# Row spread by TensorE for the first norm, later transposes, output's norms moved, and another product order in one chunk

## The chip, the core and the metric

The kernel runs on one core of one Trainium2 chip. The metric is the device time of the whole program in microseconds (us); less is better. The core has five engines with a queue of instructions each: TensorE (PE, with PEld for its weight loads), VectorE (DVE), ScalarE (ACT), GpSimd (POOL) and SyncE (SP), which here only issues DMAs. Each engine works its queue in order; an instruction that needs another engine's result or a DMA's data waits on a semaphore, and all that stands behind it in the queue waits with it.

## The reference

One layer of a decoder for 512 tokens of width 1024, fp32: FFN with half weight, token mixer, FFN with half weight, each between two RMS norms.

```python
def rms_norm(x, g):
    xf = x.astype(jnp.float32)
    y = xf * lax.rsqrt(jnp.mean(xf * xf, axis=-1, keepdims=True) + EPS)
    return (y * g.astype(jnp.float32)).astype(x.dtype)

def swiglu(h, w_gu, w_down):                 # w_gu 1024 x 5632, w_down 2816 x 1024
    gate, up = jnp.split(h @ w_gu, 2, axis=-1)
    return (jax.nn.silu(gate) * up) @ w_down
...
h = swiglu(rms_norm(x, ffn1_pre[l]), ffn1_w_gu[l], ffn1_w_down[l])
x = x + 0.5 * rms_norm(h, ffn1_post[l])
h = token_mixer(rms_norm(x, mix_pre[l]), ...)
x = x + rms_norm(h, mix_post[l])
h = swiglu(rms_norm(x, ffn2_pre[l]), ffn2_w_gu[l], ffn2_w_down[l])
x = x + 0.5 * rms_norm(h, ffn2_post[l])
```

The mixer projects to 512 pooling channels and to q (8 heads of 64), k and v (2 heads each). The pooling half takes causal means over 2, 4, 8 and 16 tokens; the attention half is causal over 128 tokens with rotary position and a sink per head. Each half is normed, and one output projection follows.

## The kernel before, in words

**Numbers.** An fp32 operand is held as two reduced fp32 parts, hi and lo: ACT copies hi (L166, L398, L438), DVE or POOL subtracts it from the source to get lo (L172, L401, L439). A product is three TensorE products, hi·hi, lo·hi and hi·lo, summed in PSUM (`mm3`, L364 to L366, and `product_late`, L480 to L483, which takes hi·lo last). PSUM has eight banks of 128 x 512 fp32.

**Tokens.** x lies in four tiles of 128 tokens. For a norm, ACT squares and sums a tile (`squares`, L358; half of it on DVE at the start, L353), DVE makes the mean (L344), POOL the root (`power`, L339), and DVE multiplies by root and gain, in two halves (`scaled`, L383). The result is called xn_a (first FFN), xn_b (mixer) and xn_c (second FFN). TensorE transposes it (tr_f L429, tr_mx L392), and ACT and DVE split the transposed tile into hi and lo.

**FFN.** The 2816 hidden columns are worked in 11 chunks of 256, gate and up together. Chunk 0 runs as eight blocks of 24 products (two token halves, gate and up, two column halves; each over two halves of the input width), called (i, kh) with i from 0 to 7. `gate_up` calls a hook, `between(i, kh)`, ahead of each half block: for the first FFN `first_steps` (L822), which norms and transposes x there, for the second `last_steps` (L1348), which runs the whole mixer and the output projection at (0, 0) and the last two transposed tiles between the blocks. Chunks 1 to 10 use seven products of half-size blocks each, numbered 1 to 7, on sums of weight blocks a, b, c, d (DVE, L224: `f_1s` = c + d and so on) and on sums of token blocks (`token_sums`, f1f and f1t). Their results go to three pairs of banks, x, y and z, taken in turn from four pairs. Then `down_proj` multiplies by w_down, again in seven products, on single banks; at its start it takes two banks for x, where chunk 10's pairs were.

**Weights.** `W` loads weights ahead over SP's queue into eight buffers and splits them into hi and lo, into a ring of six. Its list has a fixed order; `W.get` and `W.more` say when the next entries are made, and `W.put` on which engines.

**Mixer and output.** `qkv_block(t)` gives q (`pq`, 24 products of 128 x 512) and k, v (`pkv`, 24 of 128 x 256) for token tile t, with some other work between the two. `output` makes the output projection for each tile in four gathers of 12 products (`po`), adds the two halves into hm (ACT for attention, DVE L1286 for pooling), norms the sum (root r_mo, gain g4 at L1290), adds it to x (L1345) and starts the second FFN's norm (xn_c).

**Order.** TensorE's order is the order of the code throughout. Within `in_order()` this holds for DVE, ACT and POOL as well; that covers the start, the first four blocks of chunk 0 in both FFNs with all that their hooks do (so the mixer and the output too), and the down projections. Elsewhere a scheduler orders these engines, with `behind` keeping an instruction after a given one.

**Start.** SP loads tile 0 of x, the first half of the first gain, broadcast to 128 partitions (L291), tile 1, the second half, and then the first weights, with tiles 2 and 3 between them. TensorE multiplies zeros (`idle_work`, L791) until the first tile is normed.

## Time and profile before

| what | us |
|---|---|
| median of three runs | 844.01 (843.72 to 845.08) |
| the profiled execution | 843.83 |
| its span, first to last instruction | 841.9 |
| DVE busy in the span | 662.7 (79%) |
| DVE, weight splits L172 (84 of 128x1024) | 94.8 |
| mean granted clock of TensorE in the span | 0.995 |

The profile is one execution: its own time is the 843.83, and the span lies within it. Rows name line, engine, operation, output and inputs, with buffer numbers left out; "[3.54 <-DVE xn_b]" means that the engine stood idle for 3.54 us before the row, and that DVE's write of xn_b ended it. A matmul's duration is longer than the distance from one start to the next, since they are pipelined; so TensorE's pace is read from starts. The granted clock is the share of full speed that TensorE was allowed.

### The profile page before, as it was taken

Reading aid. Unit: us, or ns where it says so; the run is one execution under the profiler, and the core shown is the slowest. Engines: PE = TensorE matmul, PEld = TensorE weight load, DVE = VectorE, ACT = ScalarE, POOL = GpSimd, SP = SyncE. Lnnn points to the kernel's source line nnn. Section 1 sums busy time; section 2 is a strip of 40 time slices with the busy share of each in tenths; the row PEclk is TensorE's granted clock in tenths of the full one; section 3 lists DMA queues with packets and bytes.
Section 4 is the critical chain, followed back from the end, with each engine's and each line's share of the span. In section 5 each row is a group of like instructions: output and inputs, shape, how many; then the busy total and the mean of one; then the engine's idle time right before and its main releaser. Section 6 shows DMA issues by size and latency. Waiting matters only on the chain. (4 is left out here: it accounts for less than half of the span.)

```text
span 841.9 us, 14062 instructions
## 1 busy us (share of the span) xinstructions
PE 819.0 (97%) x5525; PEld 750.6 (89%) x5525; DVE 662.7 (79%) x856; ACT 470.1 (56%) x743; POOL 207.8 (25%) x291
## 2 busy tenths in 40 slices
PE   7999999999999999899999998999999999999996
PEld 5999999999988888788878878999999999988885
DVE  6987787777989877944766779877877778798875
ACT  6654444445556656636886467444444445566661
POOL 3103344433310000233532011133333334300001
PEclk9999999999999999999999999999999999999999
DMA  9428888988896666411005402278898888967622
GB/s 301 134 86 224 241 225 226 230 238 240 235 282 199 208 203 200 154 40 51 26 26 151 148 27 76 76 215 235 223 231 235 239 225 226 265 221 211 204 87 100
DMA packets 96877, 150.77 MB, mean 179 GB/s; under 512 B 6948, under 2 KB 53676, under 8 KB 96812
## 3 DMA queue, kind: packets, MB, share of 16 engines
q1 hardware_dynamic: 77100, 103.74, 39.3%
q0 software_dynamic: 19712, 46.15, 23.4%
q8 instruction: 43, 0.70, 0.3%
q14 instruction: 22, 0.18, 0.1%
HBM read 147.77 MB, written 48.23 MB: 233 GB/s over the span
## 5 line engine op out<-in xcount | busy, mean ns | idle before, releaser
L172 DVE TENSOR_TENSOR f_d_lo<-f_d_raw,f_d_hi 128x1024 fp32r<-128x1024 f32 x84 | 94.8, 1131 | 25.3 <-ACT f_d_hi L166 25.3
L571 POOL DMA_DIRECT2D f_t<-in_ffn_w_down x132 | 89.6, 755 | 81.7 <-issue 49.7
L166 ACT CAST f_d_hi<-f_d_raw 128x1024 fp32r<-128x1024 f32 x84 | 80.0, 979 | 26.9 <-PE f_z L366 10.6
L595 ACT COPY f_h<-f_y 128x512 f32<-128x512 f32 x20 | 11.7, 587 | 75.6 <-PE f_y L366 75.6
L568 POOL COPY f_k<-f_h 1x1 f32<-1x1 f32 x18 | 21.0, 1166 | 130.0 <-DVE f_h L560 130.0
L603 ACT ACTIVATE f_s<-f_s 128x1024 f32<-128x1024 f32 x20 | 21.2, 1060 | 41.4 <-DVE f_s L602 41.4
L571 POOL DMA_DIRECT2D f_t<-f_t x44 | 32.1, 796 | 37.8 <-issue 29.1
L600 ACT COPY f_s<-f_x 128x512 f32<-128x512 f32 x20 | 11.7, 587 | 45.1 <-PE f_x L366 45.1
L364 PE MATMUL f_x<-f_d_hi,f1e_hi 128*128 128x512 f32 x88 | 34.5, 392 | 0.7 <-DVE f_h L611 0.7
L364 PE MATMUL f_x<-f_d_hi,f2e_hi 128*128 128x512 f32 x88 | 34.4, 390 | 0.7 <-DVE f_h L611 0.7
L365 PE MATMUL f_x<-f_d_lo,f1e_hi 128*128 128x512 f32 x88 | 34.3, 389 | 0.0
L366 PE MATMUL f_x<-f_d_hi,f1e_lo 128*128 128x512 f32 x88 | 34.3, 389 | 0.0
L365 PE MATMUL f_x<-f_d_lo,f2e_hi 128*128 128x512 f32 x88 | 34.3, 389 | 0.0
L366 PE MATMUL f_x<-f_d_hi,f2e_lo 128*128 128x512 f32 x88 | 34.2, 389 | 0.0
L587 ACT COPY f_s<-f_x 128x512 f32<-128x512 f32 x20 | 11.7, 587 | 39.9 <-PE f_x L366 29.8
L637 ACT CAST f2e_hi<-f_h 128x1024 fp32r<-128x1024 f32 (+1 forms) x21 | 20.5, 979 | 20.4 <-DVE f_h L629 4.8
L637 ACT CAST f1e_hi<-f_h 128x1024 fp32r<-128x1024 f32 (+1 forms) x21 | 20.5, 980 | 20.2 <-DVE f_h L629 4.8
L339 POOL TENSOR_TENSOR r_f1po<-ms_f1po,half 128x1 f32<-128x1 f32 x4 | 2.5, 628 | 106.9 <-DVE ms_f1po L344 106.9
L339 POOL TENSOR_TENSOR r_f2po<-ms_f2po,half 128x1 f32<-128x1 f32 x4 | 2.5, 628 | 104.3 <-DVE ms_f2po L344 104.3
L364 PE MATMUL po<-wo_hi,yT_hi 128*128 128x512 f32 x64 | 25.3, 395 | 0.0
L638 DVE TENSOR_TENSOR f1e_lo<-f_h,f1e_hi 128x1024 fp32r<-128x1024 f32 (+1 forms) x21 | 23.6, 1131 | 2.1 <-ACT f1e_hi L637 2.1
L638 DVE TENSOR_TENSOR f2e_lo<-f_h,f2e_hi 128x1024 fp32r<-128x1024 f32 (+1 forms) x21 | 23.6, 1132 | 2.1 <-ACT f2e_hi L637 2.1
(1027 smaller groups left out, 3416.2 us busy)
## 6 DMA issues: line engine op xcount, KB each, us to landing
f_t<-in_ffn_w_down POOLq DMA_DIRECT2D x132, 256.0 KB, 6.4
f_d_raw<-f_t SPq DMA_DIRECT2D x40, 512.0 KB, 4.4
f_d_raw<-in_ffn_w_down SPq DMA_DIRECT2D x30, 512.0 KB, 4.3
f_t<-f_t POOLq DMA_DIRECT2D x44, 256.0 KB, 6.7
f_raw<-in_ffn_w_gu SPq DMA_DIRECT2D x8, 512.0 KB, 8.4
x<-in_x SPq DMA_DIRECT2D x4, 512.0 KB, 8.6
f_d_raw<-f_t SPq DMA_DIRECT2D x8, 256.0 KB, 3.5
wq_raw<-in_w_in SPq DMA_DIRECT2D x4, 512.0 KB, 4.0
```

The costliest lines, as they stand in the source:

```text
L166: nc.scalar.copy(hi, src)
L172: return lambda: engine.tensor_tensor(lo, src, hi.bitcast(F32), ALU.subtract)
L364: nc.tensor.matmul(ps, wh, xh, start=first, stop=False, skip_group_check=open_)
L365: nc.tensor.matmul(ps, wh, xlo, start=False, stop=False, skip_group_check=open_)
L366: nc.tensor.matmul(ps, wlo, xh, start=False, stop=last, skip_group_check=open_)
L568: then = nc.gpsimd.tensor_copy(tick, hs[(c - 1) // 4][:1, 0, (c - 1) % 4, :1]).ins
L571: nc.gpsimd.dma_start(to, part, accum_op=op, max_dma_last_dim=2048)
L587: on_act.append(nc.scalar.copy(sg[:, :, a], px[:, :, a]).ins)
L595: on_act.append(nc.scalar.copy(h[1], py[:, :, a]).ins)
L603: on_act.append(nc.scalar.activation(sg, sg, AF.Silu, scale=-1.0).ins)
L637: nc.scalar.copy(hi, src)
L638: nc.vector.tensor_tensor(lo, src, hi.bitcast(F32), ALU.subtract)
```

## The change

Four places are changed.

1. Start: the first gain comes as one row of 1024 numbers (4 KB, on ACT's DMA queue) instead of two broadcasts to 128 partitions on SP's. TensorE spreads it, as a product of a column of ones with the row, into two PSUM banks, and xn_a reads it there. 14 products of zeros become 4 ahead of this and 2 behind.
2. Chunk 1 of both FFNs: loads in the order a, b, c, d (a, c, d, b before) and products in the order 1 2 5 6 3 7 4 (1 5 2 6 3 7 4 before). The list is made up to product 5 at once behind chunk 0 (`make_to`), and in the second FFN not before the last split of a transposed tile (`hold`).
3. Mixer: block 0's pkv follows its pq at once; tile 2's transposes stand behind pq of block 1, and tile 3's behind its pkv.
4. Output: DVE's mean and root for the output norm come right behind those of the second FFN's norm, and xn_c ahead of the gain at hm; the transposes of tiles 0 and 1 are later by two gathers each, their fp32 copies (`keep`) later still; two weight splits move into `output`, with DVE in place of POOL for lo.

```diff
 SUMS = 10
-WARM = 14
+WARM = 4
...
         key = {i: f"{name}_{c}{i}" for i in ("a", "b", "c", "d", "s1")}
-        for i in "acdb":
+        for i in "abcd" if c == 1 else "acdb":
             need[i] = W.add_load(key[i], src[i], shape)
...
-        for p, last, make in (
-            (1, "a", lambda: raw[key["a"]]), (5, "d", s1), (2, "b", lambda: raw[key["b"]]),
-            (6, "b", lambda: plus("a", "s1", "a")), (3, "b", lambda: plus("b", "a", "b")),
-            (7, "b", lambda: raw[key["c"]]), (4, "b", lambda: raw[key["d"]]),
-        ):
-            W.add(f"{name}_{c}p{p}", make, need=need[last])
+        make = {
+            1: lambda: raw[key["a"]], 5: s1, 2: lambda: raw[key["b"]], 6: lambda: plus("a", "s1", "a"),
+            3: lambda: plus("b", "a", "b"), 7: lambda: raw[key["c"]], 4: lambda: raw[key["d"]],
+        }
+        last = {1: "a", 5: "d", 2: "b"}
+        for p in (1, 2, 5, 6, 3, 7, 4) if c == 1 else (1, 5, 2, 6, 3, 7, 4):
+            W.add(f"{name}_{c}p{p}", make[p], need=need[last[p]] if p in last else max(need.values()))
...
+    g1row = wk.tile([1, D], F32, tag="sg2", bufs=2, name="g1row")
+    nc.scalar.dma_start(g1row, ffn1_pre[0:1, :])
     load_x(0)
-    g1 = [slot(f"g1{n}") for n in range(2)]
-    for n in range(2):
-        nc.sync.dma_start(g1[n], ffn1_pre[0:1, n * 512 : (n + 1) * 512].to_broadcast([P, 512]))
-        if n == 0:
-            load_x(1)
+    load_x(1)
+    onerow = wk.tile([1, P], F32, tag="ra", bufs=1, name="onerow")
+    nc.vector.memset(onerow, 1.0)
+    g1 = []
     warm = cp.tile([1, 2], F32, name="warm")
...
         nc.scalar.mul(hi[:, :, at], src, -1.0)
-        nc.vector.scalar_tensor_tensor(
+        return nc.vector.scalar_tensor_tensor(
             lo[:, :, at], src, -1.0, hi[:, :, at].bitcast(F32), ALU.mult, ALU.subtract
-        )
+        ).ins
...
-    def gate_up(name, xq, hs, between):
+    def gate_up(name, xq, hs, between, hold=lambda: []):
...
         W.run_ahead = 3
-        W.more(2)
+        with behind(hold()):
+            W.make_to(W.index[f"{name}_1p5"] + 1)
...
         last = None
-        on_act, on_dve = [], []
+        on_act, on_dve = [], [done.ins]
...
                     begin = [on_act[-2], on_dve[-1]]
-            py = bank_pair(f"{name}_y{c}")
-            product(py, a, operand(f"{nm}5"), xs_[5], last=False)
-            on_act.append(nc.scalar.copy(h[1], py[:, :, a]).ins)
-            pz = bank_pair(f"{name}_z{c}")
-            product(pz, a, operand(f"{nm}2"), xs_[2])
-            on_dve.append(nc.vector.tensor_tensor(sg[:, :, a], pz[:, :, a], sg[:, :, a], ALU.add).ins)
+            for p in (2, 5) if c == 1 else (5, 2):
+                if p == 5:
+                    py = bank_pair(f"{name}_y{c}")
+                    product(py, a, operand(f"{nm}5"), xs_[5], last=False)
+                    on_act.append(nc.scalar.copy(h[1], py[:, :, a]).ins)
+                    continue
+                pz = bank_pair(f"{name}_z{c}")
+                product(pz, a, operand(f"{nm}2"), xs_[2])
+                on_dve.append(nc.vector.tensor_tensor(sg[:, :, a], pz[:, :, a], sg[:, :, a], ALU.add).ins)
             product(px, a, operand(f"{nm}6"), xs_[6], False, False)
...
     idle_work(WARM)
+    for n in range(2):
+        g1.append(bank(f"g1{n}"))
+        nc.tensor.matmul(g1[n], onerow, g1row[:, n * 512 : (n + 1) * 512], start=True, stop=True)
+    idle_work(2)
     early = {}
...
             norm1(2)
+            qkv_block(0, lambda: None)
+            qkv_out(0)
             add_to_x(3)
             size1(3)
-            qkv_block(0, lambda: turn1(2))
             root1(3)
...
         nc.gpsimd.tensor_tensor(wpl, wpr, wph.bitcast(F32), ALU.subtract)
-        qkv_out(0)
         pcols = bank("pcols")
...
         nc.vector.tensor_tensor(cols[:, 4:8], cols[:, 0:4], cols[:, 4:8], ALU.mult)
-        qkv_block(1, lambda: transposes(3, xns[3], xT2, "mx"))
+        qkv_block(1, lambda: turn1(2))
+        turn1(3)
         qkv_out(1)
...
         for kh in range(2):
-            evacuate(later[t, kh], t, kh, xq2)
+            later["evac"] = evacuate(later[t, kh], t, kh, xq2)
...
             keep(later[t, kh], t, kh, xq2)
+
+    def after(t):
+        if t:
+            root_late(t - 1)
+        later["rr"] = power(mean_square(sums[t], EPS, f"mo{t}"), f"mo{t}")
+        if t:
+            normed(t - 1)
...
                 xq2.extend(quarters("f2"))
-            if t >= 2:
-                turn_late(t - 2)
+            if t == 3:
+                turn_late(1)
             if t:
                 later["ss", t - 1] = sizes(t - 1, "c")
-            if t >= 2:
-                keep_late(t - 2)
-            pool_part(t, 1, gather(t, 1, 0), (lambda: root_late(t - 1)) if t else (lambda: None))
-            if t:
-                normed(t - 1)
-            rr = power(mean_square(sums[t], EPS, f"mo{t}"), f"mo{t}")
+            if t == 3:
+                W.more(2)
+            pool_part(t, 1, gather(t, 1, 0), lambda: after(t))
+            if t == 3:
+                lows = [W.begin(), W.begin()]
+                keep_late(0)
             for n in range(2):
...
                 nc.vector.scalar_tensor_tensor(
-                    xs[t][:, at], hm[t, n], rr, xs[t][:, at], ALU.mult, ALU.add
+                    xs[t][:, at], hm[t, n], later["rr"], xs[t][:, at], ALU.mult, ALU.add
                 )
+            if t == 2:
+                turn_late(0)
+        return lows
...
             mixer()
-            output()
+            lows = output()
             later["ss", 3] = sizes(3, "c")
+            keep_late(1)
+            for low in lows:
+                low()
             root_late(3)
-            W.put(nc.scalar, nc.gpsimd)
             normed(3)
-            W.put(nc.scalar, nc.vector)
-            W.put(nc.scalar, nc.gpsimd)
-            W.put(nc.scalar, nc.vector)
         if (i, kh) == (1, 0):
             turn_late(2)
+        if (i, kh) == (2, 0):
+            W.run_ahead = 3
+            W.more(1)
+        if (i, kh) == (3, 1):
+            turn_late(3)
             keep_late(2)
-        if (i, kh) == (3, 0):
-            turn_late(3)
             keep_late(3)
     hs2 = []
-    ends = gate_up("f2", xq2, hs2, last_steps)
+    ends = gate_up("f2", xq2, hs2, last_steps, lambda: [later["evac"]])
     g6 = gain(ffn2_post, "g6")
```

On TensorE the mixer's start reads as follows before (pq0 and pkv0 are block 0's; tr_mx20 and tr_mx21 the transposes of tile 2's halves, tr_mx30 and tr_mx31 tile 3's; three dots stand for the rest of a block):

```order
L366 MATMUL pq0_3969<-wq3_hi_3857,xT2_3_lo_3830 128x512
L392 MATMUL tr_mx20_3994<-ident_101,xn_b2_3959 128x128 x4
L392 MATMUL tr_mx21_4003<-ident_101,xn_b2_3959 128x128 x4
L364 MATMUL pkv0_4012<-wkv0_hi_3892,xT2_0_hi_3823 128x256
...
L366 MATMUL pkv0_4012<-wkv1_hi_3955,xT2_3_lo_3830 128x256
L1173 MATMUL pcols_4058<-ident_101,rows_110 128x12
L364 MATMUL pq1_4062<-wq0_hi_3742,xT2_0_hi_3823 128x512
...
L366 MATMUL pq1_4062<-wq3_hi_3857,xT2_3_lo_3830 128x512
L392 MATMUL tr_mx30_4087<-ident_101,xn_b3_4042 128x128 x4
L392 MATMUL tr_mx31_4096<-ident_101,xn_b3_4042 128x128 x4
L364 MATMUL pkv1_4105<-wkv0_hi_3892,xT2_0_hi_3823 128x256
```

and with the change (lines are numbered two to ten further on):

```order
L368 MATMUL pq0_3958<-wq3_hi_3853,xT2_3_lo_3826 128x512
L366 MATMUL pkv0_3983<-wkv0_hi_3888,xT2_0_hi_3819 128x256
...
L368 MATMUL pkv0_3983<-wkv1_hi_3951,xT2_3_lo_3826 128x256
L1183 MATMUL pcols_4036<-ident_101,rows_110 128x12
L366 MATMUL pq1_4040<-wq0_hi_3738,xT2_0_hi_3819 128x512
...
L368 MATMUL pq1_4040<-wq3_hi_3853,xT2_3_lo_3826 128x512
L394 MATMUL tr_mx20_4065<-ident_101,xn_b2_3955 128x128 x4
L394 MATMUL tr_mx21_4074<-ident_101,xn_b2_3955 128x128 x4
L366 MATMUL pkv1_4083<-wkv0_hi_3888,xT2_0_hi_3819 128x256
...
L368 MATMUL pkv1_4083<-wkv1_hi_3951,xT2_3_lo_3826 128x256
L394 MATMUL tr_mx30_4109<-ident_101,xn_b3_4030 128x128 x4
L394 MATMUL tr_mx31_4118<-ident_101,xn_b3_4030 128x128 x4
```

Block 0's pkv has moved ahead of all transposes of tile 2, which now stand where tile 3's stood.

On DVE, in `output`, from the add into x of tile 2 to the second FFN's norm of the same tile (xn_c20, xn_c21), before (ms_c2 is the mean for that norm, f2b the split transposed tile, hm31 the last pooling sum):

```order
L1345 SCALAR_TENSOR_TENSOR x2_90<-hm21_3934,r_mo2_5420,x2_90 128x512
L439 SCALAR_TENSOR_TENSOR f2b00_lo_5355<-tr_f210_5438,f2b00_hi_5354 128x4x128
L439 SCALAR_TENSOR_TENSOR f2b10_lo_5359<-tr_f211_5443,f2b10_hi_5358 128x4x128
L1286 SCALAR_TENSOR_TENSOR hm31_3935<-po130_5461,rpt_3927,hm31_3935 128x512
L344 SCALAR_TENSOR_TENSOR ms_c2_5477<-ss2_c2_5452 128x1
L1290 TENSOR_TENSOR hm31_3935<-hm31_3935,g4_3936 128x512
L383 SCALAR_TENSOR_TENSOR xn_c20_5482<-x2_90,r_c2_5479,g5_3938 128x512
L383 SCALAR_TENSOR_TENSOR xn_c21_5483<-x2_90,r_c2_5479,g5_3938 128x512
```

and with the change:

```order
L1363 SCALAR_TENSOR_TENSOR x2_90<-hm21_3930,r_mo2_5393,x2_90 128x512
L441 SCALAR_TENSOR_TENSOR f2b00_lo_5351<-tr_f200_5402,f2b00_hi_5350 128x4x128
L441 SCALAR_TENSOR_TENSOR f2b10_lo_5355<-tr_f201_5407,f2b10_hi_5354 128x4x128
L441 SCALAR_TENSOR_TENSOR f2b00_lo_5351<-tr_f210_5430,f2b00_hi_5350 128x4x128
L441 SCALAR_TENSOR_TENSOR f2b10_lo_5355<-tr_f211_5435,f2b10_hi_5354 128x4x128
L172 TENSOR_TENSOR f2_c10_lo_5454<-f2_010_raw_5235,f2_c10_hi_5453 128x4x128 x2
L1297 SCALAR_TENSOR_TENSOR hm31_3931<-po130_5459,rpt_3923,hm31_3931 128x512
L346 SCALAR_TENSOR_TENSOR ms_c2_5475<-ss2_c2_5444 128x1
L346 SCALAR_TENSOR_TENSOR ms_mo3_5479<-mss3_3939 128x1
L385 SCALAR_TENSOR_TENSOR xn_c20_5483<-x2_90,r_c2_5477,g5_3934 128x512
L385 SCALAR_TENSOR_TENSOR xn_c21_5484<-x2_90,r_c2_5477,g5_3934 128x512
L1301 TENSOR_TENSOR hm31_3931<-hm31_3931,g4_3932 128x512
```

The splits of tiles 0 and 1 (tr_f200 to tr_f211) have come together ahead of hm31, with two weight splits (f2_c10_lo) behind them, of which one was POOL's before and one stood on DVE after tile 3's xn_c; the gain at hm31 has gone behind xn_c.

On TensorE, where the second FFN's chunk 0 ends and chunk 1 begins (f2_c11 is the bank of the last block, f2_x1 the bank pair of chunk 1's product 1), before:

```order
L480 MATMUL f2_c11_5613<-f2b11_hi_5360,f2_c11_hi_5515 128x256
L481 MATMUL f2_c11_5613<-f2b11_hi_5360,f2_c11_lo_5516 128x256
L483 MATMUL f2_c11_5613<-f2b11_lo_5361,f2_c11_hi_5515 128x256 x4
L364 MATMUL f2_x1_5825<-f2b00_hi_5354,f2_1p1_hi_5779 128x256 [waits Activation_49]
L365 MATMUL f2_x1_5825<-f2b00_lo_5355,f2_1p1_hi_5779 128x256
```

and with the change:

```order
L482 MATMUL f2_c11_5615<-f2b11_hi_5356,f2_c11_hi_5488 128x256
L483 MATMUL f2_c11_5615<-f2b11_hi_5356,f2_c11_lo_5489 128x256
L485 MATMUL f2_c11_5615<-f2b11_lo_5357,f2_c11_hi_5488 128x256 x4
L366 MATMUL f2_x1_5827<-f2b00_hi_5350,f2_1p1_hi_5587 128x256 [waits DVE_49]
L367 MATMUL f2_x1_5827<-f2b00_lo_5351,f2_1p1_hi_5587 128x256
```

The order is the same; the first product of chunk 1 now waits for DVE instead of ACT.

## The prediction

> **What bounds the kernel now.** I read the page's busy times first, then TensorE's waits.
>
> ```profile
> PE 819.0 (97%) x5525; PEld 750.6 (89%) x5525; DVE 662.7 (79%) x856; ACT 470.1 (56%) x743; POOL 207.8 (25%) x291
> ```
>
> TensorE is busy for 97% of the span, and the change takes no product out of the two FFNs or the mixer. So the time can fall only where TensorE stands still or runs at a lower clock. The second view says where it waits (total, times, longest, in us):
>
> ```profile
> PE tr_f L429 <- DVE xn_a L383: 4.5, 3, 2.4
> PE tr_mx L392 <- DVE xn_b L383: 3.5, 1, 3.5
> PE tr_f L429 <- DVE xn_c L383: 1.5, 3, 0.9
> PE f_x L364 <- DVE f_h L611: 1.4, 2, 0.7
> PE f_c L483 <- DVE f2b_lo L439: 1.3, 1, 1.3
> PE f_c L481 <- POOL f_c_lo L172: 1.2, 1, 1.2
> PE f_c L483 <- DVE f1b_lo L439: 0.4, 1, 0.4
> ```
>
> Every row stands where the change works: first norm (xn_a, f1b_lo), mixer's start (xn_b), output and second FFN's chunk 0 (xn_c, f_c_lo, f2b_lo), start of each down projection (f_h L611). These seven make 13.8 us; each also costs a few tenths to refill the pipeline. I take the four places in turn, against the profiled execution's 843.83 us.
>
> **1. The start.** DVE's timeline, then TensorE's (start, duration, and in brackets the idle time before and who ended it), then windows (length, busy time of PE, PEld, DVE, ACT, POOL, granted clock, DMA share, GB/s):
>
> ```profile
> 4.42 0.69 DVE L353 CUSTOM_DVE_ANT_0 j_a<-x 128x512 f32<-128x512 f32 x1 [3.25 <-DMA x<-in_x]
> ...
> 6.52 0.75 DVE L383 SCALAR_TENSOR_TENSOR xn_a<-x,r_a,g 128x512 f32<-128x512 f32 x1 [1.11 <-DMA g<-in_ffn_pre]
> 7.93 0.69 DVE L353 CUSTOM_DVE_ANT_0 j_a<-x 128x512 f32<-128x512 f32 x1 [0.66 <-DMA x<-in_x]
> ...
> 8.75 0.16 DVE L344 SCALAR_TENSOR_TENSOR ms_a<-ss_a 128x1 f32<-128x1 f32 x1
> 9.57 2.08 DVE L383 SCALAR_TENSOR_TENSOR xn_a<-x,r_a,g 128x512 f32<-128x512 f32 x3 [0.66 <-DMA g<-in_ffn_pre]
> ```
>
> ```profile
> 10.38 2.44 PE L429 MATMUL tr_f<-ident,xn_a 128*128 128x128 f32 x12 [2.40 <-DVE xn_a L383]
> 12.67 0.58 PE L480 MATMUL f_c<-f1b_hi,f_c_hi 128*128 128x256 f32 x1
> ...
> 25.73 1.29 PE L429 MATMUL tr_f<-ident,xn_a 128*128 128x128 f32 x8 [0.82 <-DVE xn_a L383]
> ...
> 29.77 0.74 PE L483 MATMUL f_c<-f1b_lo,f_c_hi 128*128 128x256 f32 x4 [0.36 <-DVE f1b_lo L439]
> ```
>
> ```profile
> 15.00:24.90 9.90, 9.90 (x84) 9.71 (x82) 9.83 (x13) 7.10 (x18) 5.80 (x5) 1.00 0.99 311
> ```
>
> Behind tile 0's load (4.4) DVE waits three times more on a load, each time on a gain broadcast or on what is queued behind one. Without the broadcasts tile 0's first multiply needs only its root: DVE idles from 5.41, the root and its hand-offs take about 0.7 (0.73 in a row of the mixer, below), so 6.1 instead of 6.52, end 6.85. Tile 1's square sum follows at once (its load comes earlier by one broadcast, about 2 us) and takes 0.98, as from 7.93 to 8.91 before. So the three xn_a of 9.57 start at about 7.8, 1.75 earlier. From there DVE is full (9.83 of 9.90), so all it does until tile 3's norm moves up by that, and by 0.2 more for a small wait on ScalarE. TensorE waited for just this at 25.73, and its own arrival moves up as well (its first block from 12.67 to about 10.8), so it restarts 1.98 earlier. The L439 splits of tile 3, which now follow one another with one sum between, end the wait at 29.77: 0.36 and 0.2 of refill. **Term: −2.55.**
>
> What is added: a 4 KB row and two plain products of 128x512 that spread it. No product of that form is in the trace. Below, the 14 bf16 ones of that size, 0.35 each; above, four 128x128 fp32 transposes at 0.2 each in the x12 row, 0.8. I take the upper: 1.6 for both, on a TensorE with nothing else to do before the norm. The row may land as late as about 4.3. Neighbours: the first tile of x, 512 KB, is in at 4.4; the slowest small load in the list of DMA issues:
>
> ```profile
> cst<-shape_consts SPq DMA_DIRECT2D x1, 164.0 KB, 7.6
> ```
>
> That would be 8.3, cost up to 4 us of this term, and leave +1.2. Reading the gain from PSUM costs nothing: the L439 splits read PSUM too and take 0.63 each (1.89 for three in that stretch). The new order of chunk 1's products puts the split of product 6 last in DVE's backlog; row by row it is done at about 45.7, wanted at about 46.6.
>
> Now the clock, with ten of fourteen warming products gone:
>
> ```profile
> 8.00:11.40 3.40, 1.02 (x7) 0.78 (x8) 2.62 (x6) 1.59 (x4) 0.55 (x1) 1.00 1.06 352
> 11.40:14.90 3.50, 3.50 (x17) 2.92 (x15) 3.24 (x7) 3.50 (x9) 2.96 (x3) 0.51 1.07 374
> ```
>
> A stretch with 1.02 us of work in 3.40 was followed by one at 0.51 of the clock. Such a stretch can come anywhere in the changed start. Cold throughout, TensorE would reach tile 3's transposes near 23.5, and DVE has them ready at 23.6: at most 0.3 is lost. The Trainium skill, "TensorE: Matmul & The Clock Gate", Part 1, holds that a throttled clock is the default and a window of some 3.4 us of activity lifts it, which speaks against the cut of WARM; the two windows agree in length, and by the rule the sum changes by those 0.3 at most.
>
> **2. The mixer's first blocks.**
>
> ```profile
> 354.53 0.39 PE L365 MATMUL pq<-wq_lo,xT_hi 128*128 128x512 f32 x1
> 354.76 0.39 PE L366 MATMUL pq<-wq_hi,xT_lo 128*128 128x512 f32 x1
> 358.69 1.58 PE L392 MATMUL tr_mx<-ident,xn_b 128*128 128x128 f32 x8 [3.54 <-DVE xn_b L383]
> ```
>
> ```profile
> 354.36 1.22 DVE L172 TENSOR_TENSOR wkv_lo<-wkv_raw,wkv_hi 128x1024 fp32r<-128x1024 f32 x1
> ...
> 356.22 1.22 DVE L172 TENSOR_TENSOR wkv_lo<-wkv_raw,wkv_hi 128x1024 fp32r<-128x1024 f32 x1
> ...
> 364.31 2.70 DVE L383 SCALAR_TENSOR_TENSOR xn_b<-x,r_b,g 128x512 f32<-128x512 f32 x2 [0.73 <-POOL r_b L339]
> ```
>
> ```profile
> 355.14:374.32 19.18, 15.63 (x96) 14.18 (x95) 11.01 (x22) 6.19 (x18) 6.70 (x9) 0.91 0.10 29
> 359.60:363.00 3.40, 3.40 (x18) 3.40 (x17) 1.93 (x5) 2.92 (x10) 0.00 (x0) 0.50 0.01 2
> ```
>
> From the end of block 0's pq (355.14) to the start of block 2's (374.32) TensorE has 24 products of 128x512 at 0.227 from start to start (354.53 to 354.76), 48 of 128x256 at 0.120 (a block of 24 of that size in 2.87, below), 16 transposes at 0.109 (an estimate from eight of them between their neighbours) and about 0.7 of small ones: 5.45 + 5.76 + 1.74 + 0.7 = 13.65 of work in 19.18. The 5.5 lost are the wait, its refill, and the half clock that follows it. Now pkv of block 0 comes straight after pq, and needs nothing of tile 2. Late next: DVE's two wkv_lo, ready at 355.58 and 357.44, where pkv wants them at about 355.2 and 357.0: 0.4 each with a little refill, 0.9. Tile 2's transposes are due at 364.5, five after their norm; tile 3's at 368.3, and even at the old place that norm ends at 367.0. No gap is left that could drop the clock. 13.65 + 0.9 = 14.6 for 19.18. **Term: −4.55** (both wkv_lo earlier: −5.5; tile 3's norm 1.5 late: −3).
>
> **3. Output and second FFN's chunk 0.**
>
> ```profile
> 486.38:498.53 12.15, 10.83 (x53) 8.41 (x53) 9.80 (x18) 8.73 (x22) 1.65 (x3) 1.00 0.01 1
> 498.53:501.40 2.87, 2.87 (x25) 2.82 (x23) 1.93 (x5) 1.57 (x6) 0.55 (x1) 1.00 0.00 0
> 501.40:528.09 26.69, 23.54 (x187) 22.19 (x185) 24.29 (x33) 18.51 (x35) 4.04 (x4) 1.00 0.28 80
> ```
>
> The first window is 36 products of 128x512 and 16 transposes, 8.17 + 1.74 = 9.91: 2.24 lost. The second is seven blocks like the one between (24 products, 2.88) and 16 transposes, 20.16 + 1.74 = 21.9: 4.79 lost. Together 7.0. In the new order tile 0's and 1's transposes come behind two more gathers (2.72 each), when their norms are done; the first block starts at 496.3 instead of 498.53. Then tile 2 is late. Its chain in rows:
>
> ```profile
> 498.73 0.75 DVE L1286 SCALAR_TENSOR_TENSOR hm<-po,rpt,hm 128x512 f32<-128x512 f32 x1 [0.16 <-PE po L366]
> ...
> 500.94 1.41 DVE L383 SCALAR_TENSOR_TENSOR xn_c<-x,r_c,g 128x512 f32<-128x512 f32 x2
> ...
> 509.77 1.28 DVE L172 TENSOR_TENSOR f_c_lo<-f_raw,f_c_hi 128x512 fp32r<-128x512 f32 x2
> ```
>
> The last hm waits for its gather (496.3) and now for two f_c_lo ahead of it, about 498.0; then 0.7, the root with hand-offs 0.9 (0.73 and its mean before it), the first half of xn_c 0.75 and 0.25 to TensorE: 500.65. The first block ends at 499.2, so TensorE waits 1.45, longer than the 0.27 that tile 2 cost before. Behind this the splits on DVE and ScalarE are ahead of the blocks, and POOL's slow f_c_lo is gone. With 0.4 for restarts chunk 0 ends at 522.8 instead of 528.1. One wait is new: chunk 1's first product takes banks of which one holds chunk 0's last block, and DVE reads that (L542, before L539) after the block's end: one such operation and hand-offs,
>
> ```profile
> 529.07 0.67 DVE L539 SCALAR_TENSOR_TENSOR f_s<-f_c,f_s 128x512 f32<-128x512 f32 x1
> ```
>
> 0.9, between nothing (read in time) and 1.8 (one more 128x1024 ahead of it). −5.3 + 0.9: **term −4.4**, −6 if the f_c_lo are done early, −2 if ScalarE's squares keep tile 2 another two microseconds.
>
> **4. Start of both down projections.**
>
> ```profile
> 242.50 0.39 PE L366 MATMUL f_x<-f_d_hi,f1e_lo 128*128 128x512 f32 x1
> 243.57 0.50 PE L364 MATMUL f_x<-f_d_hi,f1e_hi 128*128 128x512 f32 x1 [0.68 <-DVE f_h L611]
> ```
>
> The second x bank was that of z, which DVE reads last (L611). These starts lie 1.07 apart where 0.23 is usual, and the next another 0.1 too far: 0.94. With chunk 1's product 2 ahead of 5, y and z change banks in every chunk, and the bank is now y's, read five microseconds before. Next to be late are the weight splits, in time by over a microsecond. **Term: −1.9** for the two; nothing if the banks fall otherwise.
>
> **Sum.** −2.55 − 4.55 − 4.4 − 1.9 = −13.4; 843.83 − 13.4 = 830.4. The median of the three runs is 0.2 above the profiled execution: **830.6**.
>
> **Rivals.** (a) The row is served late, landing between 4.5 and 8.3: the start's term falls to between −1.4 and +1.2, time 832 to 834.5. For it: small loads behind bulk took up to 7.6. Against: they shared SP's queue, this one has ScalarE's. The Trainium skill, "DMA: Bandwidth & Descriptors", Queues, rings and completion order, says that a DMA engine goes round its queues packet by packet, so a row on its own queue need not wait for SP's loads; no run here shows it yet. (b) Output gives only −2, time 833. For: DVE's chain there has no slack on my reckoning. (c) DVE's backlog in chunk 1 of either FFN, with less than a microsecond of slack, or the bank stays: 832 to 834. (d) Slower: the row is served only behind all of SP's loads up to chunk 1's first, at about 19.5. Then the products end at 21, the first block starts near 26 instead of 12.67, less the waits that vanish by then: +12.4, and with the other terms (−10.85) 845.4. It decides from a landing of about 18; nothing in the trace lies so long. (e) The moves don't take the waits away, terms 2 and 3 nothing: 839.4.
>
> **How the numbers follow.** Forecast 0.62, (a) 0.10, (b) 0.13, (c) 0.10, (d) 0.02, (e) 0.02, and 0.01 for a landing whose delay just eats the rest. A measurement here tells about 0.2% from no change. Faster 0.97, same 0.01, slower 0.02. Low: all four terms at −3.0, −5, −5.5 and −1.9, 828.5. High: (a), (b) and (c) reach 834.5, with a bit of two at once 835.5.
>
> **What would show it.** Right: f_c's first product near 10.8; no wait of tr_mx and no half clock after it, wkv_lo waits in its place; block 2's pq near 369.7 less the 2.5 of the start; one wait of tr_f on xn_c near 1.4 and a new one of f_x on DVE's L542; no wait on L611. Wrong: a wait of the first xn_a on the row's products, half clock beyond 15 us, a wait on a split of product 6, or a second long wait on xn_c.

## The result, and the profile after

The changed kernel takes 830.86 us (median of four runs, 830.60 to 831.20), the kernel before 843.90 in the same series: a ratio of 0.9843, with a 95% interval of 0.9826 to 0.9860. That is 13.0 us less, and the forecast was 830.6. The profiled execution took 830.70, with a span of 828.9 (841.9 before).

The page's busy times after, and TensorE's waits (total, times, longest, in us):

```profile
PE 816.6 (99%) x5521; PEld 749.8 (90%) x5521; DVE 661.2 (80%) x859; ACT 468.1 (56%) x743; POOL 209.2 (25%) x289
```

```profile
PE spare L797 <- DVE zero L791: 1.3, 1, 1.3
PE tr_f L431 <- DVE xn_c L385: 1.0, 1, 1.0
PE pt L1067 <- DVE st L1056: 1.0, 1, 1.0
PE f_x L366 <- DVE f_s L542: 0.9, 1, 0.9
PE f_x L366 <- ACT f_s L590: 0.7, 1, 0.7
PE pkv L367 <- DVE wkv_lo L172: 0.6, 2, 0.4
PE f_c L482 <- ACT f1b_hi L440: 0.3, 1, 0.3
```

The waits on xn_a, xn_b, f_h, f_c_lo, f2b_lo and f1b_lo are gone, six of the seven rows on which the prediction stood. The row on xn_c has shrunk to one wait, and the rows on wkv_lo and on L542 are the ones named in advance. The one on L590 was named by nobody, and neither was the 0.3 on f1b_hi; the rows on zero and st stood there before the change too (1.2 and 1.0). Starts of the same products in both timelines give the terms (us from the span's start):

| from, to | before | after | difference | forecast |
|---|---|---|---|---|
| span's start to first FFN's chunk 1 | 40.43 | 37.07 | −3.36 | −2.55 |
| chunk 1 to the first down projection | 201.60 | 202.60 | +1.00 | 0 |
| down projection to mixer's first pq | 107.51 | 106.53 | −0.98 | −0.94 |
| first pq to block 2's pq | 24.78 | 20.33 | −4.45 | −4.55 |
| to output's first gather | 73.40 | 73.41 | 0 | 0 |
| output to second FFN's chunk 1 | 80.37 | 75.90 | −4.47 | −4.4 |
| from there to the end | 313.81 | 313.02 | −0.79 | −0.94 |

**The start.** DVE's timeline after, then TensorE's:

```profile
6.08 0.75 DVE L385 SCALAR_TENSOR_TENSOR xn_a<-x,r_a,g 128x512 f32<-128x512 f32 x1 [0.75 <-POOL r_a L341]
...
7.63 2.15 DVE L385 SCALAR_TENSOR_TENSOR xn_a<-x,r_a,g 128x512 f32<-128x512 f32 x3
...
22.17 1.40 DVE L385 SCALAR_TENSOR_TENSOR xn_a<-x,r_a,g 128x512 f32<-128x512 f32 x2
```

```profile
3.15 3.78 PE L802 MATMUL g<-g1row,onerow 1*128 1x512 f32 x4
6.86 1.03 PE L797 MATMUL spare<-zero 128*128 128x512 bf16 x2
7.69 3.20 PE L431 MATMUL tr_f<-ident,xn_a 128*128 128x128 f32 x16
11.14 0.38 PE L482 MATMUL f_c<-f1b_hi,f_c_hi 128*128 128x256 f32 x1 [0.25 <-ACT f1b_hi L440]
```

DVE's first multiply waits for the root instead of for a load, and starts at 6.08 (forecast 6.1); the next three start at 7.63 (7.8), and chunk 0 begins at 11.14 (10.8). The spreading products begin right behind the four of zeros, at 3.15, so the row was in by then. Each of the two is two instructions, and the four take 3.78: 1.89 a product, where the forecast took 0.8. This cost nothing, since the second half of the gain was wanted at 7.63 and done at 6.9.

**The mixer**, as windows over the same products, before and then after (length, PE, PEld, DVE, ACT, POOL busy, granted clock, DMA share, GB/s):

```profile
349.54:374.32 24.78, 21.23 (x120) 18.49 (x118) 16.61 (x33) 9.74 (x26) 6.70 (x9) 0.93 0.19 64
```

```profile
346.20:366.53 20.33, 19.78 (x120) 17.15 (x118) 15.36 (x30) 8.68 (x23) 6.53 (x9) 1.00 0.25 79
```

The same 120 products; the half clock is gone with the wait.

**Output.** DVE, and TensorE behind it:

```profile
488.97 1.28 DVE L172 TENSOR_TENSOR f_c_lo<-f_raw,f_c_hi 128x512 fp32r<-128x512 f32 x2
490.17 0.74 DVE L1297 SCALAR_TENSOR_TENSOR hm<-po,rpt,hm 128x512 f32<-128x512 f32 x1
490.83 0.15 DVE L346 SCALAR_TENSOR_TENSOR ms_c<-ss_c 128x1 f32<-128x1 f32 x1
491.76 0.16 DVE L346 SCALAR_TENSOR_TENSOR ms_mo<-mss 128x1 f32<-128x1 f32 x1 [0.78 <-ACT j_mo L1299]
491.84 1.41 DVE L385 SCALAR_TENSOR_TENSOR xn_c<-x,r_c,g 128x512 f32<-128x512 f32 x2
```

```profile
492.64 0.55 PE L431 MATMUL tr_f<-ident,xn_c 128*128 128x128 f32 x3 [1.01 <-DVE xn_c L385]
...
515.84 0.39 PE L366 MATMUL f_x<-f2b_hi,f_1p_hi 128*128 128x256 f32 x1 [0.85 <-DVE f_s L542]
```

The two f_c_lo do stand ahead of hm, and tile 2's transposes wait for what follows: 1.01 where 1.45 was reckoned. Chunk 1's first product waits 0.85 for the reader of its bank.

**The wait that nobody named.** TensorE, ACT and POOL in the first FFN's chunk 1:

```profile
46.61 0.38 PE L366 MATMUL f_x<-f1t_hi,f_1p_hi 128*128 128x256 f32 x1 [0.75 <-ACT f_s L590]
```

```profile
45.98 0.58 ACT L590 COPY f_s<-f_x 128x512 f32<-128x512 f32 x1 [2.24 <-POOL f_h L545]
```

```profile
43.35 3.15 POOL L545 COPY f_h<-f_s 128x512 f32<-128x512 f32 x2 [19.95 <-DVE f1t_lo L477]
```

Read from the bottom: POOL's two copies of chunk 0's result start when DVE is through with the token sums and take 3.15; they free the buffer into which ACT copies product 1; and until that copy is done product 6 may not write product 1's bank. With the refill it costs the 1.00 in the table. The copies were not that slow in the kernel before, where DVE stood idle beside them (from 46.29 to 48.63); here DVE works on sums and splits of weights meanwhile, and the first of the two alone takes 2.6:

```profile
46.42 1.16 POOL L542 COPY f_h<-f_s 128x512 f32<-128x512 f32 x2 [21.38 <-PE f_y L366]
```

### The profile page after: what moved, and what is told of

It reads as the page before. It is cut to its first block, busy times and chain, and to the rows that moved or that the text cites. A ratio compares the mean times of both kernels' runs of the same rounds, so it can differ in the third digit from the quotient of the medians.

```text
span 828.9 us, 14054 instructions
## 1 busy us (share of the span) xinstructions
PE 816.6 (99%) x5521; PEld 749.8 (90%) x5521; DVE 661.2 (80%) x859; ACT 468.1 (56%) x743; POOL 209.2 (25%) x289
## 4 chain that ended last, share of the span: by engine, by line
PE 87%; DVE 7%; ACT 4%; issue 2%; POOL 1%; DVEq 0%; POOLq 0%; ACTq 0%
PE f_x L366 13%; PE f_x L367 13%; PE f_x L368 13%; PE f_y L366 7%; PE f_y L368 7%; PE f_y L367 7%; PE f_z L367 4%; PE f_z L368 4%; PE f_z L366 4%; PE f_c L483 1%; PE f_c L482 1%; PE f_c L485 1%; PE tr_f L431 1%; PE pq L366 1%; PE pq L367 1%
## 5 line engine op out<-in xcount | busy, mean ns | idle before, releaser
L590 ACT COPY f_s<-f_x 128x512 f32<-128x512 f32 x20 | 11.7, 586 | 36.2 <-PE f_x L368 29.8
```

What stands on the lines that cost most here:

```text
L590: on_act.append(nc.scalar.copy(sg[:, :, a], px[:, :, a]).ins)
```

## The experiments

Four kernels have one part of the change each, on the kernel before, and one has part 1 with a further edit; the others change one thing in the changed kernel, and the last one three. Times are medians; the kernel before had 844.0 to 844.4 in these series.

**Part 1 alone (start).** The row, the products that spread it, and 4 + 2 products of zeros:

```diff
-WARM = 14
+WARM = 4
...
+    nc.scalar.dma_start(g1row, ffn1_pre[0:1, :])
...
-        nc.sync.dma_start(g1[n], ffn1_pre[0:1, n * 512 : (n + 1) * 512].to_broadcast([P, 512]))
...
+        nc.tensor.matmul(g1[n], onerow, g1row[:, n * 512 : (n + 1) * 512], start=True, stop=True)
```

> The kernel before with part 1 of the change alone (row of the gain, products that spread it, 4 + 2 products of zeros), all else as before. Theory (the four parts work apart from each other): the first FFN's chunk 1 begins 2.5 to 3.4 us earlier than at 40.43, both waits on L611 stay at 0.68, the mixer's wait stays at 3.5; because the banks fall otherwise, chunk 1 of the second FFN waits up to 0.9 on DVE. Time 840.6 to 842.3. Rival (the start gains only together with the new product order): chunk 1 begins at most 2.2 us earlier, time above 842.3.

Measured 843.85, ratio 0.9995 (0.9986 to 1.0005): nothing, and both figures are those of the rival. But chunk 1 of the first FFN does begin earlier, at 38.35 instead of 40.43, 2.1 less. It is given back at two places. The first is the second FFN's chunk 1, whose first product now waits for a reader of its bank:

```profile
528.68 0.36 PE L365 MATMUL f_x<-f2b_hi,f_1p_hi 128*128 128x256 f32 x1 [1.64 <-DVE f_s L540]
```

The second is the clock in the mixer, at half for 6.8 us here where it was 3.4 before:

```profile
352.20:355.60 3.40, 0.84 (x4) 0.38 (x2) 3.15 (x6) 0.00 (x0) 1.78 (x2) 1.00 0.28 61
355.60:362.50 6.90, 5.90 (x28) 5.90 (x29) 4.51 (x10) 3.54 (x10) 1.03 (x3) 0.51 0.15 56
```

**Part 1 alone, with the bank's reader earlier.** If the bank is to blame, it is enough to finish it one block earlier:

```diff
-        for i in range(4, 8):
+        for i in (4, 5, 7, 6) if name == "f2" else range(4, 8):
...
-        for j in range(2):
+        for j in (1, 0) if name == "f2" else range(2):
```

> The kernel before with part 1 alone and the last two blocks of the second FFN's chunk 0 exchanged, with the two multiplies after them. Theory (part 1 alone gained nothing because the banks fell so that chunk 1's first product waits for the last block's reader): the wait of 1.64 on L540 falls below 0.4, time 841.8 to 842.4. Rival (its gain is lost elsewhere, in DVE's queue or to the clock): a wait of over 1 us stays there, or time above 843.

Measured 841.65, ratio 0.9976 (0.9967 to 0.9985), and the wait of 1.64 is not among TensorE's waits any more. So the start gains without the new product order, and the rival's reason was not the one. Of the 2.2 us between the two medians the profiles show 1.7 in the stretch with that bank (from output's first gather to chunk 1: 80.47 for 82.20). Chunk 1 of the first FFN begins at 37.74 in this profile, 2.7 earlier than before: the start is the same as in part 1 alone, but a root on POOL took 0.67 here and 1.80 there, and so the start's gain differs by 0.6 between the two executions.

**Part 2 alone (chunk 1's order).**

```diff
-        for i in "acdb":
+        for i in "abcd" if c == 1 else "acdb":
...
+        for p in (1, 2, 5, 6, 3, 7, 4) if c == 1 else (1, 5, 2, 6, 3, 7, 4):
```

> The kernel before with part 2 alone (chunk 1's loads and products in the new order, the list made up to product 5). Theory (the new order alone changes the banks of y and z, and so ends the waits on L611): both waits on L611 gone, -0.95 each, the f1b_lo wait of 0.36 gone, -0.5; a new wait of up to 0.9 of chunk 1's first product in the second FFN. Time 841.5 to 842.5. Rival (the banks change through the two banks that the gain takes): both waits stay, time 843.3 to 844.

Measured 841.92, ratio 0.9968 (0.9956 to 0.9979). No wait on f_h is left, so this part and not the gain's two banks moved y and z. The new bank wait is there too, longer than expected:

```profile
PE f_x L365 <- DVE f_s L541: 1.5, 1, 1.5
```

**Part 3 alone (mixer).**

```diff
+            qkv_block(0, lambda: None)
+            qkv_out(0)
             add_to_x(3)
             size1(3)
-            qkv_block(0, lambda: turn1(2))
...
-        qkv_block(1, lambda: transposes(3, xns[3], xT2, "mx"))
+        qkv_block(1, lambda: turn1(2))
+        turn1(3)
```

> The kernel before with part 3 alone (mixer). Theory: the stretch from the end of block 0's pq to block 2's pq falls from 19.2 to 14.7, no half clock in it, two waits on wkv_lo of 0.3 and 0.4 at most; time 839.2 to 839.8. Rival (tile 2's and tile 3's transposes only wait later): a wait on xn_b or on the split of a transposed tile of over 1 us in the stretch, time above 840.5.

Measured 840.41, ratio 0.9949 (0.9933 to 0.9965): less than expected. The stretch itself is as forecast, 20.28 for 24.78, with two waits on wkv_lo. But the four runs fall into two pairs, 839.80 and 839.82, and 841.00 and 841.02. The profiled one is of the second pair, and it shows a half clock in output that the kernel before didn't have, behind a stretch with 1.74 us of work in 3.30:

```profile
510.00:513.30 3.30, 1.74 (x13) 1.34 (x11) 3.30 (x5) 1.27 (x4) 0.00 (x0) 1.00 0.21 73
513.30:516.70 3.40, 3.40 (x16) 3.40 (x17) 3.40 (x6) 2.43 (x5) 0.00 (x0) 0.50 0.12 28
```

**Part 4 alone (output).**

```diff
+    def after(t):
+        if t:
+            root_late(t - 1)
+        later["rr"] = power(mean_square(sums[t], EPS, f"mo{t}"), f"mo{t}")
+        if t:
+            normed(t - 1)
...
+            pool_part(t, 1, gather(t, 1, 0), lambda: after(t))
```

> The kernel before with part 4 alone (output's norms, later transposes, weight splits). Theory: from the last gather to chunk 1 of the second FFN 4.3 to 5.3 us less, with one wait on xn_c of about 1 and up to 0.9 on DVE at chunk 1's first product; time 838.6 to 839.8. Rival (the gain in output needs the hold or the new product order of part 2): splits of token sums or of weights are late in chunk 1, over 1 us is lost there, time above 840.5.

Measured 841.88, ratio 0.9967 (0.9954 to 0.9979). The one wait of 1.02 on xn_c is there as expected, but chunk 1's first product waits 1.63 for its bank, and chunk 0 ends with a wait of 0.35 on f2b_lo. So the time is that of the rival, though the token sums were not late. By the profile output's stretch is 77.26 for 80.37, so 3.1 less where 4.3 to 5.3 were expected; the start, in which nothing was changed, was 0.7 longer in this execution.

The four parts alone give 0.2, 2.1, 3.6 and 2.1: 8.0 us, where together they give 13.0. The bank wait explains most of the difference. Parts 1, 2 and 4 bring it each by itself: from the start of chunk 0's last product to chunk 1's first they need 1.80, 1.67 and 1.79 more than the 0.12 of before, 5.3 in all. Together they bring it once, 1.01. That is 4.3 of the 5.0; the rest is of the size of the half clocks that the remaining waits bring in, lies within the intervals of the five medians (about 1 us each), and was not taken apart further.

**The changed kernel with the mixer as before.** The diff is part 3's, reversed.

> The changed kernel with the mixer as before, parts 1, 2 and 4 changed. Theory (part 3 is worth what its own stretch says, 4.45, and its wait drops the clock for 3.4 or 6.8 us, depending on where it falls in the windows of the clock): the wait of 3.5 on xn_b is back with half clock behind it; time 835.2 to 836.3. Rival (part 3 is worth only what it gave by itself, 3.6 against the kernel before, or less): time below 834.6.

Measured 834.78, ratio 0.9895 (0.9879 to 0.9910): 3.9 above the changed kernel, between the two expectations. The stretch is 24.60, with a half clock of 3.4, so 4.27 above 20.33. The forecast's 4.55 for part 3 is somewhat too much, and 3.6 too little.

**The gain in SBUF.** The start gained 0.8 more than forecast, and tile 3's two multiplies took 1.40 where they had taken 2.45. Both profiles have a split of POOL's beside them, but in the changed kernel the gain lies in PSUM. Their rows in the kernel before, POOL's first:

```profile
23.05 1.99 POOL L172 TENSOR_TENSOR f_c_lo<-f_raw,f_c_hi 128x512 fp32r<-128x512 f32 x1
```

```profile
23.80 2.45 DVE L383 SCALAR_TENSOR_TENSOR xn_a<-x,r_a,g 128x512 f32<-128x512 f32 x2
```

The edit gives tiles 2 and 3 a copy of the gain in SBUF:

```diff
+            for n in range(2):
+                nc.scalar.copy(kept_g1[n], g1[n])
...
+        early["x", t] = scaled(t, early["r", t], g1 if t < 2 else kept_g1, "a", between)
```

> The changed kernel, but tiles 2 and 3 of the first norm read the gain from a copy in SBUF (two copies by ScalarE) instead of from PSUM. Theory (DVE's multiply with all operands in SBUF is slowed while GpSimd works on a weight split, and with the gain in PSUM it is not): the two multiplies of tile 3 take 2.4 instead of 1.40, TensorE waits 0.8 to 1.0 for them, chunk 1 begins 0.8 to 1.0 later than 37.07; time 831.3 to 831.9. Rival (they were fast for another reason, such as the new order around them): 1.40 as before, no wait, time as the changed kernel, 830.9.

Measured 834.11, ratio 0.9874 (0.9858 to 0.9891). The multiplies of tile 3 took 2.43, but the time missed both expectations: the copies held up ACT's first split, chunk 0 began at 12.54 instead of 11.14, and the clock was at half until 15.6. So the place was changed: copies just ahead of tile 3, for that tile alone.

```diff
             size_of(3)
+            for n in range(2):
+                nc.scalar.copy(kept_g1[n], g1[n])
...
+        early["x", t] = scaled(t, early["r", t], g1 if t < 3 else kept_g1, "a", between)
```

> The changed kernel, but tile 3 alone of the first norm reads the gain from SBUF, copied by ScalarE late, just ahead of it, where ScalarE has a gap, so that nothing before tile 3 moves (the run before this one with copies for tiles 2 and 3 also held up the first splits on ScalarE). Theory (operands all in SBUF are slowed by GpSimd's split, a gain in PSUM is not): first product of chunk 0 at 11.1 to 11.3 as in the changed kernel, the two multiplies of tile 3 take 2.4 instead of 1.40, chunk 1 begins 0.8 to 1.1 later than 37.07; time 831.5 to 832.0. Rival (the copies, not the place of the gain, cost the time in that run): 1.40 as before, chunk 1 within 0.3 of 37.07, time 830.6 to 831.2.

Measured 831.96, ratio 0.9857 (0.9841 to 0.9874), as the theory had it. POOL's split beside tile 3 in the changed kernel, where the multiplies took 1.40 (22.17, above), then the split and the multiplies of this run with the gain from SBUF (g1s), and TensorE behind them:

```profile
21.50 1.89 POOL L172 TENSOR_TENSOR f_c_lo<-f_raw,f_c_hi 128x512 fp32r<-128x512 f32 x1
```

```profile
21.71 1.89 POOL L172 TENSOR_TENSOR f_c_lo<-f_raw,f_c_hi 128x512 fp32r<-128x512 f32 x1
```

```profile
22.38 2.43 DVE L385 SCALAR_TENSOR_TENSOR xn_a<-x,r_a,g1s 128x512 f32<-128x512 f32 x2
```

```profile
24.20 0.55 PE L431 MATMUL tr_f<-ident,xn_a 128*128 128x128 f32 x3 [1.05 <-DVE xn_a L385]
```

The place of the gain alone is not slow: in the run before this one tile 2's multiplies read it from SBUF too, with no instruction of POOL beside them:

```profile
19.57 1.41 DVE L385 SCALAR_TENSOR_TENSOR xn_a<-x,r_a,g1s 128x512 f32<-128x512 f32 x2
```

It takes both, the gain in SBUF and POOL at work. Chunk 1 begins at 38.31 for 37.07, 0.2 of which was lost before tile 3. So one us of what the start saved comes from where the gain lies.

**Output's two f_c_lo later.**

```diff
-            if t == 3:
-                W.more(2)
             pool_part(t, 1, gather(t, 1, 0), lambda: after(t))
             if t == 3:
+                W.more(2)
                 lows = [W.begin(), W.begin()]
```

> The changed kernel, with output's two f_c_lo (and their hi) behind the norm of tile 2 instead of ahead of the last hm. Theory (these two on DVE are what makes tile 2's transposes late): the wait of 1.01 on xn_c falls below 0.2, nothing else waits longer, time 829.6 to 829.9. Rival (ScalarE's squares or the root hold tile 2): a wait of 0.5 or more stays on xn_c, time above 830.2.

Measured 829.87, ratio 0.9824 (0.9808 to 0.9840). The wait on xn_c is gone from the list, nothing else waits longer. The two splits were the cause; their hi on ACT moved with them, but DVE's row shows hm right behind the two f_c_lo, without idle time.

**Chunk 0's last two blocks exchanged**, the edit shown above, in the changed kernel:

> The changed kernel, with the last two blocks of the second FFN's chunk 0 exchanged and DVE's two multiplies after them likewise, so that the bank that chunk 1's first product takes is read 2.9 us earlier. Theory (that bank is the wait): the wait of 0.85 on f_s (L542) is gone, time 829.7 to 830.0. Rival (DVE's queue is late whatever bank it is): a wait of 0.4 or more stays at chunk 1's first product, or another takes its place, time above 830.4.

Measured 830.55, ratio 0.9832 (0.9812 to 0.9852). The wait on L542 is gone, but 0.32 comes back at once as a second wait on L590, in the second FFN, where product 6 is now wanted earlier. And in the profiled run 0.6 was lost at the start, where POOL's root took 1.80 instead of 0.67. So the time is that of the rival, and a smaller wait did take the place of the old one. Yet the bank was the wait at chunk 1's first product: the stretch from output's first gather to it is 74.85 for 75.90.

**Chunk 0's copies on ScalarE.**

```diff
-            nc.gpsimd.tensor_copy(hs[0][:, 2 * j : 2 * j + 2, 0], sg)
+            nc.scalar.copy(hs[0][:, 2 * j : 2 * j + 2, 0], sg)
```

> The changed kernel, with the two copies of chunk 0's result (L545) on ScalarE instead of GpSimd, in both FFNs. Theory (ScalarE's copy of product 1 waits for the buffer that GpSimd's slow copies free, and TensorE's product 6 waits for it): the wait of 0.75 on L590 in the first FFN is gone, time 829.7 to 830.1. Rival (ScalarE itself or the split of product 6 is late there): a wait of 0.4 or more stays before product 6, time above 830.4.

Measured 829.73, ratio 0.9825 (0.9809 to 0.9842). The wait on L590 is gone, and chunk 1 to the first down projection takes 201.60 again, as in the kernel before. Three of the runs took 829.71 to 829.75, the profiled one 830.69, and its windows say why: the clock fell to half behind the old wait of 0.96 in the mixer.

```profile
424.30:427.70 3.40, 2.44 (x19) 1.92 (x17) 1.51 (x6) 2.87 (x8) 0.38 (x1) 1.00 0.02 5
427.70:431.10 3.40, 3.40 (x9) 2.65 (x9) 1.68 (x3) 3.34 (x8) 2.17 (x5) 0.50 0.00 0
```

**The three together.**

> The changed kernel with the three edits together: the two f_c_lo behind the norm of tile 2, the last two blocks of chunk 0 exchanged, chunk 0's copies on ScalarE. Theory (three waits of TensorE apart from each other): waits of 1.01, 0.85 and 0.75 gone, with their refills 3.2 us in all, time 827.6 to 828.1 if no half clock comes in. Rival (a stretch at half clock after the wait of 0.97 on L1056, as in the run with the copies alone, or a new wait on L590 in the second FFN): 0.5 to 1.5 given back, time 828.2 to 829.3.

Measured 827.54 (827.29 to 827.96), ratio 0.9809 (0.9794 to 0.9824): faster than the changed kernel, 3.3 by the medians, which is just beyond the lower end of the theory. Here the same wait, at the same place, left the clock alone:

```profile
424.30:427.70 3.40, 2.44 (x18) 1.97 (x18) 1.51 (x6) 2.87 (x9) 0.44 (x1) 1.00 0.02 5
427.70:431.10 3.40, 3.33 (x14) 2.34 (x15) 1.73 (x3) 3.34 (x9) 2.12 (x5) 1.00 0.00 0
```

What TensorE still waits for, three rows in all:

```profile
PE spare L797 <- DVE zero L791: 1.3, 1, 1.3
PE pt L1067 <- DVE st L1056: 1.0, 1, 1.0
PE pkv L367 <- DVE wkv_lo L172: 0.6, 2, 0.4
```

## Why the prediction was right, and where it was not

**Where TensorE stands still.** This reading held: the seven rows made the gain, and the stretch in which nothing was changed kept its length to 0.01 us (73.40 and 73.41).

**The start: right in kind, off in size, and the total came right by a miss the other way, which was luck.** It gave 3.36 for 2.55, and chunk 1 took 1.00 of it back, for nothing forecast. The step that failed is "From there DVE is full (9.83 of 9.90), so all it does until tile 3's norm moves up by that". DVE was full, but its last operation also got shorter, 1.40 for 2.45, because its second operand had moved to PSUM; of that move the prediction said "Reading the gain from PSUM costs nothing", and it did not ask what the move would save. Rival (a) and the slower rival (d) fell with the row's arrival before 3.15. The clock went to full at 10.3 and stayed there through the stretch where it had been at half before, better than the forecast's 0.3 lost.

**Chunk 1: the rival was in the right place with the wrong link.** Rival (c) put the risk in chunk 1, at DVE's split of product 6, "done at about 45.7, wanted at about 46.6". It was done at 45.5 and wanted at 45.7, so in time by less than reckoned; but POOL's copies and ACT's copy of product 1, which the prediction did not follow, were later still, and cost the 1.00. The run with the copies on ACT shows that link by taking it away.

**The mixer.** −4.45 for −4.55, with the waits on wkv_lo at 0.38 and 0.18 for 0.4 each. Undone in the changed kernel it is worth 3.9 to 4.3.

**Output.** −4.47 for −4.4, and for the reasons given: the f_c_lo ahead of hm (shown by moving them) and the bank of chunk 0's last block (shown by exchanging the blocks). The sizes were 1.01 for 1.45 and 0.85 for 0.9.

**The down projections.** Both waits went, 0.98 and 0.79 for 0.94 each, and part 2 alone does it, as said.

**The sum as a sum.** The prediction added four terms as if each were there without the others. They are not: alone they make 8.0. That the whole came out is because the whole change has the bank wait once, which the prediction counted once, and no half clock at all.

## What to carry to other kernels

When several waits are removed from an engine that is nearly full, work the terms out on the final order, not on one edit at a time: a single edit can be worth nothing because it moves a bank or the clock against you, and three such edits together pay that price once. Where a chain of engines frees a buffer, follow it to its end, also through the engines with the most idle time; here it was the idlest one, GpSimd, that made TensorE wait as soon as TensorE was three microseconds early.

## What the runs showed of the hardware

**An operand in PSUM takes DVE out of GpSimd's way.** Two 128x512 multiplies of x by root and gain took 2.43 with x and gain in SBUF while POOL worked on a split, 1.40 with the gain in PSUM and the same split beside them, and 1.41 with the gain in SBUF and POOL idle. It goes the other way as well: POOL's two copies of 128x512 took 1.16 while DVE stood idle, and 3.15 while DVE worked on sums and splits of weights. The Trainium skill, "SBUF — State Buffer", Who interferes with whom, says that a DVE instruction with two SBUF inputs contends with a GpSimd instruction that reads SBUF, and one with at most one SBUF input doesn't, outside of the faster modes. These runs agree, and it would have given the missing microsecond of the first term in advance.

**A wait of one microsecond can cost two, or not.** Behind the wait of 0.96 on L1056 the clock fell to half for 3.4 us in one kernel (the profiled run with the copies on ACT, +0.95 against its other three runs) and not in another that issues the same work there within 0.1 us of it. In the trace's record of the granted clock, the full-speed stretch ahead of that drop is 416.4 us, and so it is in the first run with the gain in SBUF; in the profiles of before, of part 1 alone and of the mixer undone it is 344.7. These are 122 and 101 times 3.413. The Trainium skill, "TensorE: Matmul & The Clock Gate", Part 1, has a window of 3413 ns that runs on whatever the kernel does. The runs agree with that, and go beyond its rule of thumb, idle gaps of over 3.4 us: a gap of 0.96 with transposes behind it was enough. TensorE in the run that dropped:

```profile
425.50 1.47 PE L1067 MATMUL pt<-ident,st 128*128 128x128 f32 x8 [0.96 <-DVE st L1056]
426.80 0.95 PE L1101 MATMUL oss<-ones,osq 128*128 128x1 f32 x8
427.62 0.72 PE L366 MATMUL pu<-xT_hi,wu_hi 128*128 128x512 f32 x1
```

With the wait, 3.1 us go by here without a large product. Where they lie in the windows can be counted from where the clock last rose. In this run a window goes from 424.3 (11.26 + 121 x 3.413) to 427.7 and holds nearly all of them, and 0.3 us of large products. In the kernel with all three edits a border at 425.1 (12.1 + 121 x 3.413) cuts them, and each window has 1.0 or more of large products. All fourteen profiles of this case have this wait, at 0.95 to 0.97. The clock fell in the two in which a window had only 0.3 and 0.5 of large products (the second is the first run with the gain in SBUF), and stayed in the twelve in which each had 0.9 or more. So the place of the border, which differs from execution to execution, seems to decide; two drops are few to prove it.

The half clock of part 3 alone, in output, fits this: both waits there (0.29 and 1.27) lie in one window, with 1.9 of work in its 3.4, while in the kernel before a border at 516.6 cuts the longer one and leaves 2.7 and 2.6 of work in the two windows. A window with 1.9 of work was not enough there, so 0.9 is no general limit. How much work a window must have, and of what kind, is not settled.
